# Keys and values in pieces within the attention of the first pair of head groups, the second pair's queries in DRAM

## The chip, the cores and the metric

The kernel runs on one core of one Trainium2 chip. A core has a matrix engine (TensorE, PE in the profile, with its weight loads as PEld), three other engines (VectorE: DVE, ScalarE: ACT, GpSimd: POOL), a queue engine that only issues transfers here (SyncE: SP), an on-chip memory (SBUF), and eight banks of accumulators (PSUM) that PE writes and that DVE and ACT read. Each engine runs its instructions in the order of its own list and waits at semaphores for the others. The metric is the device time of one launch in microseconds; lower is better.

## The reference, cut to what matters

One inference step of a trunk of two layers over T = 1056 tokens (1024 of a prompt, 32 of a sample), D = 1024. Layer 0 is an mLSTM with an MLP. Layer 1 is an attention over chunks of 64 tokens with an MLP. The change lies in that attention: 16 query heads in 4 groups, each group with one head of keys and values of 64 numbers. A chunk sees itself and the 8 chunks before it; the sample sees 512 cached keys and its own 32.

```python
kv = (x * (1 + kv_scale) + kv_shift) @ p['w_kv']          # 1024 -> 512
k_sh = kv[..., :KV_W].reshape(Bsz, S, NKV_B, HD_B)        # KV_W = 4 groups * 64
v_sh = kv[..., KV_W:].reshape(Bsz, S, NKV_B, HD_B)
q = (u @ p['w_q_b'][lb]).reshape(Bsz, S, NH_B, HD_B)      # 16 heads * 64
def one_chunk(args):                                       # prompt, per chunk ci
    s = jnp.einsum('bqkgd,bskd->bkgqs', qb, kb) * (HD_B ** -0.5) + bias
    s = jnp.where(valid, s, -jnp.inf)
    p = jax.nn.softmax(s, axis=-1)
    return jnp.einsum('bkgqs,bskd->bqkgd', p, vb)
...
y = o @ p['w_out_b'][lb]
```

The newest 512 keys and values of the prompt and the 32 of the sample are outputs as well (`k_p`, `v_p`, `k_s`, `v_s`).

## The kernel before, in words

Everything is float32. A product of two float32 matrices is made of three matmuls in a faster format: each operand is split into a high part (a cast by ACT, L89) and the rest (a subtraction by DVE, L90), and high·high, high·low and low·high are added up in PSUM (`proj`, L118 to L120).

**Queries (L1414 to L1440).** The tokens come in three blocks `TBS` of 384, 384 and 288. In two passes (column blocks `pr` 0, 1, 2, then 3) each block runs 24 matmuls for each of the `fc` of the pass (8 in all: two heads each) and splits the result by ACT (L1439) and DVE (L1440) into `QO`, one SBUF tile for each block. A block's inputs come out of a layer norm whose steps (`norms[ti]`, ACT L889 to L891 and L326 among them) run during the block ahead of it. `QO` later takes the attention's output in the queries' place.

**Keys and values (L1443 to L1527).** A phase of its own: 9 tiles of 128 tokens (`NT`; the last has 32). For a tile a transfer brings x (L1482), POOL multiplies (L1487), DVE adds (L1488), ACT and DVE split (L89, L90) into `uk`, and PE runs 24 matmuls for the keys and 24 for the values, in two PSUM banks (L1509 to L1511). Values are copied out by ACT (L1515). Keys go through `put_keys` (L1456 to L1467): a split (ACT L1456, DVE L1457), four transposes on PE into a bank `kt` (L1462), and eight casts out of that bank into the key tiles `k`, four by ACT for the high part and then four by DVE for the low part (L1467). Four tiles of cached keys go the same way (`kt_c`). In this phase the PSUM banks are in rotation for all of it.

**Attention (L1530 to L1660).** Head groups go in two pairs, `gp` 0 and 1. For a pair, 17 chunks (chunk 16 is the sample) come in an order that alternates wide and slim ones, and each chunk has two groups `e`. A softmax unit (`softmax_unit`) is the scores `s` on PE (L1558; 8 matmuls of 288 columns for a full chunk and group, in two units), bias and minimum by DVE (L1569), the exponential by ACT (L1572), a reciprocal by DVE (L1573) and the scaling by POOL (L1574). `transposed` turns the rows on PE into up to three banks `pt` (L1588), copied out to `pT` by DVE for e = 0 (L1598) and by ACT for e = 1 (L1596). `weighted_values` makes 20 matmuls `pv` (L1608) and writes the split result to `QO` (ACT L1613, DVE L1614). PSUM here: `s` 2 buffers of 2 banks, `pt` 3 buffers, `pv` 1. The position bias comes by transfers at the start of the attention (L1541, L1545).

**Order.** `Flow.tick` interleaves generators: a group's scores come three steps ahead of its transposes, and these one ahead of `pv`. On PE this order is taken as written (`manual_schedule`); on the other engines a scheduler sets a fixed order when the program is built.

Of the kernel before, what the change touches and what calls it, by code (L numbers as in the profile page):

```python
# [15 lines left out]
P = 128  # L16
# [59 lines left out]
def trunk_kernel(ctx: ExitStack, tc: tile.TileContext, a, o):  # L76
# [1332 lines left out]

    qo_cm, QOT = [], []  # L1410

    def qo(c):
        return QOT[c // 6][:, :, :, c % 6, :]
    wq = a["w_q_b"][0]  # L1414
    for gi, grp in enumerate(((0, 1, 2), (3,))):
        ws = {pr: [wblock(f"q{pr}_{half}", wq, 512 * half, 256 * pr) for half in range(2)] for pr in grp}
        for ti, (t0, n) in enumerate(TBS):
            if gi == 0:
                flow.finish(norms[ti])
                acc_cm[ti].__exit__(None, None, None)  # L1420
                qo_cm.append(tc.tile_pool(name=f"qo{ti}", bufs=1, reuse_waits="tile"))
                QOT.append(qo_cm[ti].__enter__().tile([P, 2, 2, 6 if ti < 2 else 5, 256], F32R, name=f"QO{ti}"))
                if ti == 2:
                    nc.vector.memset(qo(16)[:, :, :, 128:256].bitcast(F32), 0.0)
            for fc in [f for pr in grp for f in (2 * pr, 2 * pr + 1)]:
                g, r = fc // 2, 2 * (fc % 2)
                gp, e = g // 2, g % 2
                ps = mm(f"q_{fc}_{t0}")
                proj(ps[:, :n], n, ws[fc // 2], fc % 2, lambda hl, k: uap(hl, k, t0, n))
                for hd in range(2):  # L1430
                    for off, m, cnd in segs(t0, n):
                        if cnd == 0:
                            dst = QOT[ti][:, e, gp, 0:m // 64, (r + hd) * 64:(r + hd + 1) * 64]
                            src = ps[64 * hd:64 * hd + 64, off:off + m].rearrange("p (c i) -> p c i", i=64)
                        else:
                            dst = qo(16)[:, e, gp, (r + hd) * 32:(r + hd + 1) * 32]
# [5 lines left out]
    up_cm.__exit__(None, None, None)  # L1442

# [5 lines left out]
    wkv = [[wblock(f"kv{pr}_{half}", a["w_kv"], 512 * half, 256 * pr) for half in range(2)] for pr in range(2)]  # L1449
# [3 lines left out]
    def put_keys(src, m, pos, nm):  # L1453

        kd = [tmp_t([P, 256], f"kd{i}_{nm}", F32R) for i in range(2)]
        nc.scalar.copy(kd[0][:m], src)  # L1456
        nc.vector.tensor_sub(kd[1][:m], src, kd[0][:m].bitcast(F32))  # L1457
        yield
        ps = bank(f"kt_{nm}").rearrange("p (i b t) -> p i b t", i=2, b=2)
        for i in range(2):  # L1460
            for b in range(2):
                nc.tensor.transpose(ps[:, i, b, :m], kd[i][:m, b * P:(b + 1) * P].bitcast(F32), ident[:m, :m])  # L1462
        for i in range(2):
            for g0 in range(2):
                for half in range(2):
                    dst = kk[i][64 * half:64 * half + 64, g0::2, pos:pos + m]
                    KCOPY[i][half != g0](dst, ps[64 * g0:64 * g0 + 64, i, :, :m])  # L1467

# [23 lines left out]
    uks = [kv_input(0), kv_input(1)]  # L1492

    def cached_keys(t):
        cr = tmp_t([P, 256], f"ck_{t}")
        nc.sync.dma_start(cr, ck[t * P:(t + 1) * P])
        nc.sync.dma_start(V[:, 8 + t], cv[t * P:(t + 1) * P])
        yield 3.0
        yield from put_keys(cr, P, TP + t * P, f"c{t}")
    for t in range(NT):  # L1500
        if t % 2 == 0 and t < 8:
            flow.add(cached_keys(t // 2))
        m = P if t < NT - 1 else TS
        uk = uks[t]
        pk = [bank(f"kv{i}_{t}")[:, :256] for i in range(2)]
        for i in range(2):
            for k in range(KC):
                w = wkv[i][k // 4]
                nc.tensor.matmul(pk[i], uk[:, 0, k], w[:, 0, k % 4], start=(k == 0), stop=False)  # L1509
                nc.tensor.matmul(pk[i], uk[:, 0, k], w[:, 1, k % 4], start=False, stop=False)  # L1510
                nc.tensor.matmul(pk[i], uk[:, 1, k], w[:, 0, k % 4], start=False, stop=(k == KC - 1))  # L1511
            if i == 0:
                flow.tick()
        vi = t if t < NT - 1 else 12
        nc.scalar.copy(V[:m, vi], pk[1][:m])  # L1515
        flow.add(put_keys(pk[0][:m], m, t * P if t < NT - 1 else TP + 512, f"n{t}"))
        flow.tick()
        if t >= 4:
            ks = tmp_t([P, 256], f"ks_{t}")
            nc.scalar.copy(ks[:m], pk[0][:m])  # L1520
            dk, dv = (o["k_p"], o["v_p"]) if t < NT - 1 else (o["k_s"], o["v_s"])
            r0 = (t - 4) * P if t < NT - 1 else 0
            nc.sync.dma_start(dk[0, r0:r0 + m].rearrange("s g d -> s (g d)"), ks[:m])
            nc.sync.dma_start(dv[0, r0:r0 + m].rearrange("s g d -> s (g d)"), V[:m, vi])
        if t + 2 < NT:
            uks.append(kv_input(t + 2))
    flow.finish()  # L1527
    ps0.__exit__(None, None, None)


    at_cm = tc.tile_pool(name="attn", bufs=1, reuse_waits="tile")
    at = at_cm.__enter__()
    psT_cm = tc.tile_pool(name="psT", bufs=1, space=PSUM, reuse_waits="tile")
    psT = psT_cm.__enter__()
    bias, sbias = [], []
    for i, (nb, ns) in enumerate(((3, 0), (3, 0), (2, 1), (0, 3))):
        bt = ring.tile([P, 2112], F32, tag="wc", name=f"bias{i}", bufs=6)
        b3 = bt[:, :nb * 576].rearrange("p (b j) -> p b j", j=576) if nb else None
        for hd in range(2 if nb else 0):
# [7 lines left out]
        bias += [b3[:, j] for j in range(nb)]  # L1547
        sbias += [s3[:, j] for j in range(ns)]

    nun = [0]  # L1550

    def softmax_unit(qst, g, k0, nk, bt, off, nm):
# [3 lines left out]
        for b, j0, w in parts:  # L1556
# [3 lines left out]
        i = nun[0] % 12  # L1560
        p = tmp_t([P, 640], f"p_{nm}") if i < 5 else raw_tile([P, 640], f"p_{nm}") if i < 8 else \
            at.tile([P, 640], F32, tag="p", name=f"p_{nm}", bufs=4)
# [14 lines left out]
    def transposed(ps_, wid, e, nm):  # L1577
# [4 lines left out]
        for j0 in range(0, nt, 2):  # L1582
            pt = psT.tile([P, 2, 256], F32, tag="pt", name=f"pt_{nm}_{e}_{j0}", bufs=3)
            js = range(j0, min(nt, j0 + 2))
            for j in js:
# [7 lines left out]
            for j, m, kp in jss:  # L1593
                dst, src = pt_sb[:kp, j:j + m, :nq], pt[:kp, j - j0:j - j0 + m, :nq]
                if e:
                    nc.scalar.copy(dst, src)  # L1596
                else:
                    nc.vector.tensor_copy(dst, src)  # L1598
        return pt_sb
# [16 lines left out]
    def att_group(gp, c, e):  # L1616
# [3 lines left out]
        if c < 16:  # L1620
# [4 lines left out]
            pr_ = [softmax_unit(qo(c)[:, e, gp, pr * P:(pr + 1) * P], g, k0, nk, bias[2 * g + pr][:, 576 - nk:], off,  # L1625
                                f"{nm}_{e}{pr}") for pr in range(2)]
        else:
            wid, vt0 = 544, 8
            pr_ = [softmax_unit(qo(16)[:, e, gp, 0:P], g, TP, 544, sbias[g], 0, f"{nm}_{e}")]
        yield  # L1630
        yield
        yield
        pts[gp, c, e] = transposed(pr_, wid, e, nm)
        yield
        if e:
            if c < 16:
                dst = lambda hl: qo(c)[:, hl, gp, :]
            else:
                dst = lambda hl: qo(16)[:, hl, gp, :].rearrange("p (r i) -> p r i", i=64)[:, :, :TS]
            weighted_values(gp, [pts[gp, c, i] for i in range(2)], len(pr_) * P, wid, vt0, dst, nm)  # L1640
    pts = {}
# [8 lines left out]

    wide, slim = (8, 12, 13, 14, 15, 9, 10, 11), ((7, 6, 5, 4, 16, 3, 2, 1, 0), (16, 7, 6, 5, 4, 3, 2, 1, 0))
    with tc.manual_schedule(engines={mybir.EngineType.PE}):
        for gp in range(2):
            for i in range(17):
                c = slim[gp][i // 2] if i % 2 else wide[i // 2] if i < 16 else slim[gp][8]
                for e in range(2):
                    flow.add(att_group(gp, c, e))
                    flow.tick()  # L1660
                if gp and i in (8, 11):
                    wo_pre[0, len(wo_pre)] = wo_block(0, len(wo_pre))
        flow.finish()
    psT_cm.__exit__(None, None, None)
# [36 lines left out]
    def o_mov(hl, k, ti):  # L1701
        return QOT[ti][:, hl, k // 4, :, (k % 4) * 64:(k % 4 + 1) * 64]
# [96 lines left out]
```

## Time and profile before

| | |
|---|---|
| time, median of 3 runs | 2478.24 us (2475.82 to 2480.36) |
| the profiled execution's own time | 2479.81 us |
| its span in the trace | 2478.0 us |
| mean granted clock of PE | 0.992 |
| busy share of the span | PE 97%, PEld 93%, DVE 71%, ACT 41%, POOL 7% |
| queries, 1264 to 1359.2 us | 95.2 us, PE busy 94.5 |
| keys and values, 1359.2 to 1421.8 us | 62.6 us, PE busy 58.5 |
| attention, 1421.8 to 1632 us | 210.2 us |
| first scores of the second pair | at 1529.7 us |

The stages follow each other in time, so a window of the trace is a stage. "Busy" of PE counts a pipelined matmul from its start to its modelled end, so that a busy PE isn't yet a PE at its best pace. The idle time of an engine that isn't the one that sets the end costs nothing. A releaser is the instruction of another engine for which a wait ended.

### The profile page before, as it was taken

Reading aid. Unit: us, or ns where it says so; the run is one execution under the profiler, and the core shown is the slowest. Engines: PE = TensorE matmul, PEld = TensorE weight load, DVE = VectorE, ACT = ScalarE, POOL = GpSimd, SP = SyncE. Lnnn points to the kernel's source line nnn. Section 1 sums busy time; section 2 is a strip of 40 time slices with the busy share of each in tenths; the row PEclk is TensorE's granted clock in tenths of the full one; section 3 lists DMA queues with packets and bytes.
Section 4 is the critical chain, followed back from the end, with each engine's and each line's share of the span. In section 5 each row is a group of like instructions: output and inputs, shape, how many; then the busy total and the mean of one; then the engine's idle time right before and its main releaser. Section 6 shows DMA issues by size and latency. Waiting matters only on the chain.

```text
span 2478.0 us, 42688 instructions
## 1 busy us (share of the span) xinstructions
PE 2413.7 (97%) x16844; PEld 2315.4 (93%) x16844; DVE 1759.7 (71%) x4038; ACT 1016.9 (41%) x2118; POOL 168.6 (7%) x315
## 2 busy tenths in 40 slices
PE   7999999999999999999999999999999999999997
PEld 4999999999999999999999867789999999899997
DVE  4899999788679679677597667746853442776758
ACT  4644456382211212212266556654754443221212
POOL 0211100000000000000001134410000000000003
PEclk9999999999999999999999989999999999999999
DMA  8433224313224224234122310050375646767632
GB/s 297 122 110 101 84 88 129 107 35 119 77 87 137 84 86 135 80 92 142 43 98 82 91 40 1 18 147 27 134 251 212 215 179 254 262 239 273 255 130 72
DMA packets 236220, 318.10 MB, mean 128 GB/s; under 512 B 11624, under 2 KB 185084, under 8 KB 234996
## 3 DMA queue, kind: packets, MB, share of 16 engines
q1 hardware_dynamic: 236020, 315.38, 38.8%
q8 instruction: 132, 2.16, 0.4%
q14 instruction: 68, 0.56, 0.1%
HBM read 242.79 MB, written 74.91 MB: 128 GB/s over the span
## 4 chain that ended last, share of the span: by engine, by line
PE 78%; DVE 8%; DMA 6%; ACT 2%; issue 1%; POOL 0%; SPq 0%; DVEq 0%; POOLq 0%; ACTq 0%
PE up L118 10%; PE up L120 10%; PE up L119 9%; PE dn L1283 9%; PE dn L119 5%; PE dn L118 5%; PE dn L120 5%; DMA fx<-hd 3%; PE pv L1608 2%; PE pt L1588 2%; PE s L1558 2%; PE o L118 1%; PE o L119 1%; PE o L120 1%; PE op_b L118 1%
## 5 line engine op out<-in xcount | busy, mean ns | idle before, releaser
L120 PE MATMUL up<-u,w_up 128*128 128x264 f32 x1024 | 292.9, 286 | 0.0
L118 PE MATMUL up<-u,w_up 128*128 128x264 f32 x1024 | 292.4, 286 | 0.0
L119 PE MATMUL up<-u,w_up 128*128 128x264 f32 x1024 | 291.1, 284 | 0.0
L1283 PE MATMUL dn<-fx,wf 128*128 128x264 f32 x2208 | 275.3, 286 | 7.9 <-DMA fx<-hd 7.4
L1283 PEld LDWEIGHTS dn<-fx,wf 128*128 128x128 f32 x2208 | 272.2, 189 | 9.7 <-issue 4.6
L119 PE MATMUL dn<-h,w_dn 128*128 128x384 f32 (+1 forms) x768 | 249.5, 325 | 0.0
L118 PE MATMUL up<-U,w_up 128*128 128x384 f32 (+1 forms) x768 | 249.2, 324 | 0.0
L119 PE MATMUL up<-U,w_up 128*128 128x384 f32 (+1 forms) x768 | 247.9, 323 | 0.0
L118 PE MATMUL dn<-h,w_dn 128*128 128x384 f32 (+1 forms) x768 | 247.8, 323 | 0.0
L120 PE MATMUL up<-U,w_up 128*128 128x384 f32 (+1 forms) x768 | 247.6, 322 | 0.0
L120 PE MATMUL dn<-h,w_dn 128*128 128x384 f32 (+1 forms) x768 | 247.3, 322 | 0.0
L119 PEld LDWEIGHTS up<-u,w_up 128*128 128x128 f32 x1024 | 193.9, 189 | 0.0
L118 PEld LDWEIGHTS up<-u,w_up 128*128 128x128 f32 x1024 | 193.8, 189 | 0.0
L120 PEld LDWEIGHTS up<-u,w_up 128*128 128x128 f32 x1024 | 193.3, 189 | 0.0
L986 DVE SCALAR_TENSOR_TENSOR ACC<-dn,ada,ACC 128x264 f32<-128x264 f32 (+4 forms) x328 | 131.7, 426 | 86.4 <-PE dn L1283 74.6
L238 DVE SCALAR_TENSOR_TENSOR aacc<-rada,cs,aacc 128x256 f32<-128x256 f32 x448 | 190.3, 477 | 0.0
L986 DVE SCALAR_TENSOR_TENSOR acc<-dn,ada,acc 128x384 f32<-128x384 f32 (+2 forms) x256 | 119.4, 486 | 47.4 <-PE dn L120 46.3
L1025 ACT ACTIVATE r<-up 128x384 f32<-128x384 f32 (+1 forms) x96 | 44.3, 463 | 246.9 <-PE up L120 238.4
L119 PEld LDWEIGHTS dn<-h,w_dn 128*128 128x128 f32 x768 | 144.4, 188 | 0.2 <-DVE h L1028 0.2
L120 PEld LDWEIGHTS dn<-h,w_dn 128*128 128x128 f32 x768 | 144.5, 188 | 0.0
L120 PEld LDWEIGHTS up<-U,w_up 128*128 128x128 f32 x768 | 144.3, 188 | 0.0
L118 PEld LDWEIGHTS up<-U,w_up 128*128 128x128 f32 x768 | 144.2, 188 | 0.1
(354 smaller groups left out, 5957.4 us busy)
## 6 DMA issues: line engine op xcount, KB each, us to landing
hd<-HL SPq DMA_DIRECT2D x28, 1848.0 KB
raw_up<-in_w_up_dram SPq DMA_DIRECT2D x68, 512.0 KB
rada<-in_w_ada_dram SPq DMA_DIRECT2D x64, 512.0 KB
fx<-hd SPq DMA_DIRECT2D x37, 528.0 KB
raw_dn<-in_w_down_dram SPq DMA_DIRECT2D x36, 512.0 KB
ada_room<-in_w_ada_dram SPq DMA_DIRECT2D x32, 512.0 KB
fx<-hd SPq DMA_DIRECT2D x50, 264.0 KB
fx<-hd SPq DMA_DIRECT2D x16, 792.0 KB
```

What stands on the lines that cost most here:

```text
L118: nc.tensor.matmul(ps, wh, mov(0, k), start=(k == 0), stop=False)
L119: nc.tensor.matmul(ps, wh, mov(1, k), start=False, stop=False)
L120: nc.tensor.matmul(ps, wl, mov(0, k), start=False, stop=(k == nk - 1))
L238: nc.vector.scalar_tensor_tensor(acc[:, cnd], raw[:, k], sc, acc[:, cnd], op0=ALU.mult, op1=ALU.add)
L986: nc.vector.scalar_tensor_tensor(xs, ps[:, off + o:off + o + mm_], gate[:, fc, cnd:cnd + 1], xs, op0=ALU.mult, op1=ALU.add)
L1025: nc.scalar.activation(r, ps[:, :n], AF.Relu)
L1283: nc.tensor.matmul(p, ws[w][:, wl, k], t[:, s0, xl], start=first and k + n_ == 0, stop=k == kg - 1 and n_ == 2, skip_group_check=not first)
L1558: nc.tensor.matmul(s[:, b, :w], qst, kk[i][:, g, k0 + j0:k0 + j0 + w], start=(i == 0), stop=(i == 1))
L1588: nc.tensor.transpose(pt[:kp, j - j0, pr * P:(pr + 1) * P], ps_[pr][:, j * P:j * P + kp], ident)
L1608: nc.tensor.matmul(pv[64 * e:64 * e + 64, :nq], V[:kp, vt0 + j, g * 64:(g + 1) * 64], pts[e][:kp, j, :nq], start=(j == 0), stop=(j == nt - 1))
```

## The change

The two passes of the queries take the column blocks 2, 3, 0 and then 1, so that the second pair's queries (`fc` 4 to 7) are ready first in each block. `QO`'s layout puts the pair first. After `fc` 7 of each block the second pair's half of `QO` is written to DRAM (`qd`, 1.57 MB, 1.57 MB and 1.31 MB), and that half's room then holds the split weights of the keys and values. The phase of keys and values is gone: its matmuls come from a generator in pieces of 6, and each `put_keys` is a piece as well. 18 pieces (tiles 0 and 1) are placed ahead of the attention; the rest is handed out at three places per group in the first pair, 0.75 of a piece each, and ahead of a chunk whose keys are still missing. Both halves of a tile's result, keys and values, lie in one bank `KVB`. The transposes of keys share the buffers `pt` with the attention's, two while there are pieces left, three after. The first pair goes through its chunks from 0 up; the second pair keeps its order. When the pieces are at an end, `second_pair` loads the queries back and brings two further bias tiles; at the start only two are loaded.

```diff
     def qo(c, gp):
+        return QOT[c // 6][:, gp, :, c % 6, :]
-    for gi, grp in enumerate(((0, 1, 2), (3,))):
+    for gi, grp in enumerate(((2, 3, 0), (1,))):
...
+                if fc == 7:
+                    nc.sync.dma_start(qd[ti], QOT[ti][:, 1].bitcast(F32))
                 flow.tick(n / 96)
+            if gi:
+                if ti == 0:
+                    r0 = rooms(0, 3)
+                    kv_block(0, 0, r0[0:2])
+                elif ti == 1:
+                    r1 = rooms(1, 3)
+                    kv_block(0, 1, r1[0:2])
+                    kv_block(1, 0, (r0[2], r1[2]))
+                else:
+                    kv_block(1, 1, rooms(2, 2))
...
+    KVB = psX_cm.__enter__().tile([P, 2, 256], F32, name="KVB")
...
     def put_keys(kd, m, pos, nm):
-        ps = bank(f"kt_{nm}").rearrange("p (i b t) -> p i b t", i=2, b=2)
+        ps = psT.tile([P, 2, 256], F32, tag="pt", name=f"kt_{nm}", bufs=2).rearrange("p i (b t) -> p i b t", b=2)
...
+    def kv_tile(t):
...
+        for i in range(2):
+            pk = KVB[:, i]
+            for k in range(KC):
+                w = wkv[i, k // 4]
+                nc.tensor.matmul(pk, uk[:, 0, k], w[0][:, k % 4], start=(k == 0), stop=False)
+                nc.tensor.matmul(pk, uk[:, 0, k], w[1][:, k % 4], start=False, stop=False)
+                nc.tensor.matmul(pk, uk[:, 1, k], w[0][:, k % 4], start=False, stop=(k == KC - 1))
+                if k % 2 == 0:
+                    continue
+                if k == KC - 1 and i == 0:
+                    work = raw_tile([P, 4, 256], f"kd_{t}")
+                    kd = kd_of(work)
+                    split_keys(kd, pk[:m], m)
...
+                elif k == KC - 1:
+                    nc.scalar.copy(V[:m, vi], pk[:m])
...
+                    if t + 2 < NT:
+                        uks[t + 2] = kv_input(t + 2)
+                yield
+                if k == 3 and i == 1:
+                    put_keys(kd, m, pos, f"n{t}")
+                    yield
...
+    fills = [0, 18.0]
+    def fill(share):
...
+        fills[1] += share
+        while fills[0] < fills[1]:
+            if next(pieces, fill) is fill:
+                fills[0] = None
+                return
+            fills[0] += 1
...
+            if psY and nun[1] % 3 == 0:
+                pt = psY[0].tile([P, 2, 256], F32, tag="pt3", name=f"pt_{nm}_{e}_{j0}", bufs=1)
+            else:
+                pt = psT.tile([P, 2, 256], F32, tag="pt", name=f"pt_{nm}_{e}_{j0}", bufs=2)
             js = range(j0, min(nt, j0 + 2))
+            if j0 == 4:
+                fill(0.75)
...
+    def second_pair():
+        psX_cm.__exit__(None, None, None)
...
+        for ti in range(3):
+            nc.sync.dma_start(QOT[ti][:, 1].bitcast(F32), qd[ti])
+        bias_tile(2)
+        bias_tile(3)
...
-    wide, slim = (8, 12, 13, 14, 15, 9, 10, 11), ((7, 6, 5, 4, 16, 3, 2, 1, 0), (16, 7, 6, 5, 4, 3, 2, 1, 0))
+    order = tuple(range(17)), (8, 16, 12, 7, 13, 6, 14, 5, 15, 4, 9, 3, 10, 2, 11, 1, 0)
```

Three places in the engines' lists show what moved. A row has the line, the operation, what it writes and what it reads; a number behind a name tells buffers of one name apart.

The first place is PE in the first pair, where the keys of tile 6 (`kt_n_15372`) are put. Of the changed kernel:

```order
L1550 MATMUL KVB<-QO_13199,uk_14907 128x256
L1501 MATMUL kt_n_15372<-ident,kd_15303 128x128 x4
L1671 MATMUL pt_9_1_0_15386<-ident,p_9_10_15227 128x128
L1671 MATMUL pt_9_1_0_15386<-ident,p_9_11_15239 128x128
...
L1671 MATMUL pt_9_1_2_15392<-ident,p_9_10_15227 128x128
L1671 MATMUL pt_9_1_2_15392<-ident,p_9_11_15239 128x128
...
L1548 MATMUL KVB<-QO_13709,uk_14907 128x256
```

`kt`, `pt_9_1_0` and `pt_9_1_2` follow each other and share two buffers, so the third needs the buffer of the first; before, the key transposes stood among the matmuls of the key and value phase and had banks of that phase.

The second place is ACT at the same point, in the changed kernel: the exponentials of chunk 10, the four casts of the high part of tile 6's keys, then chunk 9's copies.

```order
L1649 ACTIVATE p_10_10_15349,mx_10_10_15350<-p_10_10_15349,mx_10_10_15350 128x576
L1649 ACTIVATE p_10_11_15360,mx_10_11_15361<-p_10_11_15360,mx_10_11_15361 128x576
L1506 CAST k_14124<-kt_n_15372 64x2x128 x4
L1679 COPY pT_9_1_15385<-pt_9_1_0_15386 128x512
L1493 CAST ck_15515<-ck_15515 128x256
L1679 COPY pT_9_1_15385<-pt_9_1_2_15392 128x512
```

Before, ACT had in the middle of the first pair only exponentials, `pT` copies and the writes to `QO`; now the casts of keys stand between two exponentials and the copies out of `pt`.

The third place is ACT in the queries, at the end of the layer norm of the third block. Before:

```order
L889 ACTIVATE w_n_2_13415<-var_n_2_13412,eps_ln 128x288
L1439 CAST QO_13196<-q_0_13440 64x6x64
L890 ACTIVATE w_n_2_13415<-w_n_2_13415 128x288
L891 ACTIVATE w_n_2_13415<-w_n_2_13415 128x288
```

and now:

```order
L889 ACTIVATE w_n_2_13419<-var_n_2_13416,eps_ln 128x288
L1458 CAST QO_13199<-q_0_13444 64x6x64
L890 ACTIVATE w_n_2_13419<-w_n_2_13419 128x288
L89 CAST QO_13199<-raw_kv_0_13979 128x1024
L891 ACTIVATE w_n_2_13419<-w_n_2_13419 128x288
```

The cast of a weight block into the room of the queries that go to DRAM now stands ahead of the norm's last step; it writes where the transfer to `qd` still reads.

More of the change, by code (lines that the diff above doesn't have):

```diff
@@ L1494, in cached_keys @@
     def cached_keys(t):
-        cr = tmp_t([P, 256], f"ck_{t}")
-        nc.sync.dma_start(cr, ck[t * P:(t + 1) * P])
+        work = raw_tile([P, 4, 256], f"ck_{t}")
+        nc.sync.dma_start(work[:, 2], ck[t * P:(t + 1) * P])
         nc.sync.dma_start(V[:, 8 + t], cv[t * P:(t + 1) * P])
[L1498 to L1526, printed above, removed]
@@ L1660, in trunk_kernel @@
                     flow.tick()
+                    if fills[0] is None and not psY:
+                        second_pair()
                 if gp and i in (8, 11):
```

125 lines of the change are left out of this document (92 added, 33 removed).

## The prediction

> **What bounds the kernel now.** I read first the stretches of the stages around the change (a row is a stretch, its length, and each engine's busy time with its instructions in brackets, then the granted clock of PE and the load on the transfers).
>
> ```profile
> core 0: us, PE busy (x) PEld busy (x) DVE busy (x) ACT busy (x) POOL busy (x), PEclk, DMA share, GB/s
> 1264.00:1359.20 95.20, 94.47 (x580) 93.01 (x580) 77.50 (x142) 62.32 (x134) 7.24 (x3) 1.00 0.30 94
> 1359.20:1421.80 62.60, 58.50 (x486) 57.55 (x485) 42.86 (x79) 34.31 (x88) 12.09 (x6) 1.00 0.35 91
> 1421.80:1440.00 18.20, 11.71 (x52) 8.88 (x51) 10.41 (x35) 8.87 (x25) 5.71 (x8) 0.70 0.65 149
> 1440.00:1480.00 40.00, 39.67 (x283) 29.29 (x282) 28.04 (x92) 24.51 (x67) 15.79 (x30) 0.96 0.00 1
> 1480.00:1520.00 40.00, 38.87 (x303) 29.06 (x302) 28.30 (x99) 26.18 (x75) 17.30 (x34) 1.00 0.01 1
> ```
>
> PE sets the end in all five, and only the attention's first 18.2 us stand out: 52 matmuls, at a clock of 0.70, where the next 40 us hold 283. The chain of work that ended last says why, and finer stretches show the clock behind it.
>
> ```profile
> 1423.54 6.78 DMA bias<-bias_d
> ```
>
> ```profile
> 1425.00:1430.00 5.00, 2.93 (x10) 2.04 (x10) 1.93 (x9) 2.50 (x6) 2.20 (x3) 0.58 1.02 223
> 1430.00:1435.00 5.00, 3.70 (x14) 3.23 (x15) 2.21 (x8) 2.39 (x6) 1.42 (x2) 0.50 1.02 228
> 1435.00:1440.00 5.00, 3.27 (x18) 2.37 (x17) 3.22 (x10) 2.90 (x7) 2.09 (x3) 0.84 0.07 18
> ```
>
> The transfer of the bias holds the first softmax up, and the clock then stays low for ten microseconds. The third view is the waits: in the key and value phase, and then from 1440 to 1530 us, the rest of the first pair.
>
> ```profile
> PE kv L1511 <- DVE uk L90: 4.1, 4, 2.1
> ```
>
> ```profile
> PEld s L1558 <- DVE mx L1569: 5.3, 15, 0.6
> PEld pt L1588 <- POOL p L1574: 3.5, 9, 0.4
> PEld pt L1588 <- DVE pT L1598: 2.0, 6, 0.4
> PE s L1558 <- DVE mx L1569: 1.2, 5, 0.3
> ```
>
> PE's own work, which the change leaves as it is, by the chain's steps of undisturbed matmuls and two rows of the timeline:
>
> ```profile
> 1375.20 0.12 PE kv L1509
> 1375.92 0.44 PE kt_c L1462 x4
> 1376.36 0.44 PE kt_n L1462 x4
> ...
> 1445.57 1.07 PE s L1558 x8
> 1446.64 0.87 PE pt L1588 x8
> ```
>
> ```profile
> 1504.24 2.38 PE L1608 MATMUL pv<-pT,V 128*64 128x256 f32 x20
> 1529.74 1.33 PE L1558 MATMUL s<-k,QO 128*128 128x288 f32 x8 [0.34 <-DVE mx L1569]
> ```
>
> Keys and values: 432 x 0.12 + 52 x 0.11 = 57.5 us. A pair, half of the 400 s, 500 pt and 520 pv of the attention: 200 x 0.134 + 250 x 0.109 + 260 x 0.119 = 85 us. The second row is the second pair's first scores: up to there, keys, values and the first pair took 1359.2 to 1529.7, 170.5 us, beside 143 of work. So 27 us are the most that this part can give.
>
> **What the change can give.** *The attention's start.* At the pace of the next row (283 matmuls in 40 us, 7.1 in a microsecond) 52 matmuls would take 7.3 us and not 18.2: 10.9 us. The two bias tiles are now issued in the queries, and key and value matmuls stand ahead of the first softmax. I count 11 (from 7, if the first softmax is late in its turn, to 12). *The waits of the key and value phase*: 4, PE's wait above. *The first pair's small waits*: the windows show 1.5 us of PE not busy in 80; the four rows of waits add up to 12.0, part of it under a matmul that still runs. Between 1.5 and 12 I take 8, near the upper end, since a late weight load also spreads the matmuls that count as busy. Gain: 11 + 4 + 8 = 23 us, if the pieces of keys and values fill these places and bring no waits with them.
>
> **What the change costs.** *The queries.* ACT's cast into the room of the written-out queries stands ahead of the last step of the third block's norm, and has to wait until the 1.57 MB to DRAM have been read. At the 228 GB/s of the row above that is 7 us from its issue. Before, the step came here:
>
> ```profile
> 1301.83 0.45 ACT L891 ACTIVATE w_n<-w_n 128x288 f32<-128x288 f32 x1
> ```
>
> ```profile
> PE q L118 <- ACT U L326: 0.2, 1, 0.2
> ```
>
> Queued behind the cast are that step and then all of the third block's inputs, which PE already waits for by 0.2 us, so that no slack covers it. Nought, if the transfer is issued by 1295, to 6; I take 2. The other transfers added to the queries run under PE's matmuls.
>
> *The start of keys and values.* Both halves of a tile now share a bank, so PE has to wait for the copies out of it, where it had another bank before. The groups of instructions of the phase (mean ns behind the comma):
>
> ```profile
> L1457 DVE TENSOR_TENSOR kd_n<-kv,kd_n 128x256 fp32r<-128x256 f32 (+1 forms) x9 | 3.8, 424 | 3.2 <-ACT kd_n L1456 3.0
> L1456 ACT CAST kd_n<-kv 128x256 fp32r<-128x256 f32 (+1 forms) x9 | 3.4, 373 | 20.1 <-DVE kd_c L1457 8.8 <-PE kv L1511 4.5 <-PE kt_c L1462 4.5
> L1515 ACT COPY V<-kv 128x256 f32<-128x256 f32 (+1 forms) x9 | 3.4, 373 | 3.2 <-PE kv L1511 3.2
> ```
>
> Between keys and values of a tile stand 0.37 + 0.42 us and two hand-overs, about 1.0; between values and the next keys 0.37 and its hand-overs, about 0.6. Up front nothing lies between: two of the first and one of the second, 2.6 us. The first softmax stands on DVE behind four key casts and a split (1.7 and 1.2 us by the rows below), of which I count 2.4. Together 5 (2 to 8). For the seven later tiles attention lies between most pieces: 7 x 1.6 = 11 us at most, of which I count 3 (0 to 7).
>
> *The keys among the transposes.* This is the largest term. The timeline of ACT and DVE (casts in a row are one row, with their time together), and one group:
>
> ```profile
> 1376.45 1.50 ACT L1467 CAST k<-kt_c 64x256 fp32r<-64x256 f32 x4
> 1377.97 1.51 ACT L1467 CAST k<-kt_n 64x256 fp32r<-64x256 f32 x4
> 1380.71 1.22 DVE L90 TENSOR_TENSOR uk<-x,uk 128x1024 fp32r<-128x1024 f32 x1
> 1382.30 1.72 DVE L1467 CAST k<-kt_c 64x256 fp32r<-64x256 f32 x4
> ```
>
> ```profile
> L1467 DVE CAST k<-kt_n 64x256 fp32r<-64x256 f32 x29 | 12.2, 421 | 2.1 <-ACT k L1467 1.8
> ```
>
> A bank of key transposes is read by ACT for 1.50 us, and then by DVE for 1.72: DVE's idle time ahead of its casts ends on ACT's. With a hand-over the bank is held 3.4 us from the end of the transposes; here kt_c was held from the end of its transposes at 1376.36 (the chain's row above) to 1384.02, over 7 us, because DVE was late, and it hurt nobody, since the phase had its other banks. Now two buffers serve keys and attention alike: the second bank behind the keys' is the keys' own again. PE has four transposes to do in between (0.44) and at some places six key and value matmuls (0.72), 0.4 to 1.2 us in all, and so waits 2.2 to 3.0 us if ACT begins at once. Where the exponentials of the next chunk stand ahead on ACT, they come on top, with their read-out:
>
> ```profile
> 1504.72 0.78 ACT L1572 ACTIVATE p<-p,mx 128x576 f32<-128x576 f32 x1
> 1505.40 0.19 ACT L1572 ACTIVATION_READ_ACCUMULATOR p<-p,mx 128x1 f32 x1
> ```
>
> Against it, in the early chunks the pieces and groups are small, and where the keys take the third bank of a group its scores and pv lie behind. Eleven such places are in the first pair (tiles 2 to 8 and four cached ones; the last tile has 32 tokens). Ten times 2.0 is 20 us; 6, if PE finds half a microsecond of wait at each, and 40, if two exponentials stand ahead at every one, are the ends.
>
> [...]
>
> *Two buffers for transposes, not three.* A copy out takes 0.55 us on DVE (mean) against 0.44 of transposes:
>
> ```profile
> L1598 DVE COPY pT<-pt 128x512 f32<-128x512 f32 (+3 forms) x82 | 42.9, 554 | 8.9 <-PE pt L1588 8.8
> ```
>
> The third bank of a group comes 0.3 us early unless a piece lies ahead, as it does at most groups; and DVE's casts make some copies late. 3 (1 to 8). *The hand-over.* 4.45 MB and two bias tiles (2.1 MB, worked out from their shapes as floats) come once the last piece is done. At 223 GB/s the first queries that are needed take 7 us and all of it 29; the second pair's first scores stand a chunk and a half of the first pair (8 to 10 us) and its bias later. I take 2 (0 to 10). Reads and writes of the outputs are in both versions.
>
> Costs: 2 + 5 + 3 + 20 + 3 + 2 = 35. Less the 23 gained: **+12 us**. On the profiled execution's own 2479.8 that is 2491.8; this execution was 1.6 us above the median, so on the median's scale **2490 us**.
>
> **Rivals.** *The fill works (faster).* The pieces cover the key casts, because PE comes to the third bank late anyway: then the keys cost 6, the shared bank 1, buffers 2, the start 3, queries and hand-over 1: 13 - 23 = -10, 2468 us. For it speaks that the attention's waits in the table are single ones of at most 0.6 us, against it that PE works in order and that ACT's casts are sandwiched between exponentials. It decides from below 0.7 us of wait per key place. *It evens out.* Key places at 0.8 us, 8 in all: 35 - 12 - 23 = 0, 2478 us. *DVE becomes the bound (slower).* The groups of DVE in the whole attention:
>
> ```profile
> L1569 DVE CUSTOM_DVE_ANT_0 p<-s,bias 128x576 f32<-128x576 f32 (+9 forms) x132 | 77.2, 604 | 16.2 <-PE s L1558 13.0 <-DMA bias<-bias_d 2.4 <-issue 0.3
> L1573 DVE RECIPROCAL mx<-mx 128x1 f32<-128x1 f32 x132 | 20.7, 160 | 29.2 <-ACT p L1572 27.8
> ```
>
> With copies (42.9), the writes to QO and the read-outs (24.2) they make 165 us, half of it for a pair; 82 + 43 of keys and values is 125 us beside 143 of PE. Against the 170.5 us of before: at the 71% that DVE shows in the attention's stretches 125 us take 176, and with the start, queries and hand-over (9) that is 185, +14; but if DVE's casts wait for ACT as its rows show (2.1 us of idle time ahead of 29 casts, 3.2 ahead of 9 splits) while its reductions wait behind them, 68% is nearer: 184 + 9, +22, 2500 us. It decides where PE's waits end on DVE's reductions and not on casts. *The reload isn't hidden (slower).* The first scores of the second pair wait 8 us more for the queries or the bias, and as after the bias stall above the clock falls (10.9 us were lost there for a wait of 6.8): +12 + 8, 2498 us. [...]
>
> **How the numbers follow.** The forecast has 0.38, the fill that works 0.24, evened out 0.17, DVE 0.12, the reload 0.09. About 0.2%, 5 us, is what a measurement of this kernel can tell from no change. The forecast's own range, 2482 to 2505, is the key places at 1.2 to 3.3 us. Over all, 8 in 10 lie between 2464 and 2506: down to the fill that works with a small rest, up to forecast and reload together. Faster 0.24, the same 0.18, slower 0.58.
>
> **What would show it.** Right: from the end of the queries to the second pair's first scores it takes about 180 us (before 170.5; PE's work is 143); in it PE waits for the casts out of kt (L1506) or for the copies behind them (L1679), some ten times, 1 to 4 us each; the start shows no bias wait and a full clock; the second pair keeps its 102 us. Wrong: PE's waits of that kind add up to under 8 us (then it's faster), or most of them end on DVE's reductions, or PE stands still ahead of the second pair's first scores.

## The result and the profile after

The changed kernel takes 2521.0 us (median, 2519.3 to 2525.4), the kernel before beside it 2479.3: four runs each, a ratio of 1.0173, with a 95% interval of 1.0155 to 1.0190. The forecast was slower, 2490 us in a range of 2464 to 2506. The sign was right; the time lies 15 us above the range, and the loss is 42 us where 12 were worked out.

The span grew from 2478.0 to 2519.3 us, and the trace says in which stage. The table counts from the first matmul of one stage to the first of the next, in the profiled executions, and the out-projection from its first matmul to its last; the attention's second pair starts with its 201st scores matmul. The median of all runs of a kernel stands beside it. The experiments stand in it as well, since they are read from it.

| profiled execution | queries | keys, values, first pair | second pair | out-projection | median us |
|---|---|---|---|---|---|
| before | 95.7 | 170.4 | 102.3 | 95.6 | 2479 |
| changed | 96.0 | 198.3 | 113.7 | 97.1 | 2521.0 |
| e1 softmax buffers | 96.0 | 199.6 | 105.0 | 95.6 | 2510.7 |
| e2 all ahead | 95.9 | 183.8 | 113.8 | 95.6 | 2505.7 |
| e3 low key casts left out | 96.0 | 186.7 | 114.4 | 97.2 | 2510.5 |
| e4 phase, with rooms | 95.8 | 156.9 | 102.2 | 95.6 | 2468.3 |
| e5 high key casts left out | 96.0 | 180.6 | 116.1 | 95.6 | 2503.7 |
| e6 cover | 95.9 | 186.0 | 115.2 | 95.6 | 2504.5 |
| e7 later input | 96.0 | 197.6 | 113.5 | 97.1 | 2518.9 |
| e8 rooms, rising order | 95.9 | 153.2 | 104.6 | 95.6 | 2467.9 |
| e9 = e1 + e6 | 95.9 | 182.2 | 104.7 | 95.6 | 2497.4 |
| e10 one bank in the phase | 95.9 | 178.9 | 102.3 | 95.6 | 2488.1 |

So +27.9 lie in keys, values and first pair, +11.4 in the second pair, which was to keep its time, +1.5 in the out-projection and +0.3 in the queries. First the stretches of the changed kernel (columns as in the prediction; the last row lies in the second pair).

```profile
core 0: us, PE busy (x) PEld busy (x) DVE busy (x) ACT busy (x) POOL busy (x), PEclk, DMA share, GB/s
1360.00:1380.00 20.00, 14.69 (x106) 14.08 (x105) 8.27 (x13) 5.83 (x16) 3.81 (x2) 0.91 0.30 80
1380.00:1400.00 20.00, 16.20 (x111) 14.10 (x110) 13.22 (x53) 11.82 (x40) 6.29 (x13) 0.91 0.21 54
...
1420.00:1440.00 20.00, 15.49 (x92) 11.90 (x93) 11.70 (x31) 9.51 (x26) 6.76 (x9) 0.83 0.06 16
...
1480.00:1500.00 20.00, 15.26 (x108) 12.56 (x106) 12.62 (x33) 11.46 (x30) 3.96 (x7) 0.91 0.07 21
...
1600.00:1640.00 40.00, 36.26 (x246) 26.48 (x244) 27.15 (x91) 22.68 (x64) 14.19 (x29) 0.91 0.12 27
```

No single stretch stands out as the attention's start did before. PE is idle for a tenth to a quarter of the time in nearly every stretch of the first pair, no other engine is busier than PE, and the granted clock is under 1 again and again. The waits of PE from 1390 us to the second pair's first scores, the five largest rows (what waits, what ended the wait, then us in total, how many, the longest):

```profile
PE pt L1671 <- ACT pT L1679: 14.5, 7, 3.2
PE pt L1671 <- DVE pT L1681: 4.4, 6, 1.6
PE KVB L1548 <- ACT kd L1558: 3.8, 2, 2.3
PE KVB L1548 <- DVE kd L1494: 1.7, 2, 1.2
PE pt L1671 <- DVE k L1506: 1.4, 2, 0.9
```

The first row is the place that the prediction named: transposes that wait for a buffer whose copy on ACT stands behind the casts of keys. One such place in the timeline, at tile 4's keys, shows the chain whole:

```profile
1451.99 0.66 PE L1501 MATMUL kt_n<-ident,kd 128*128 128x128 f32 x4
...
1452.68 0.74 ACT L1506 CAST k<-kt_n 64x256 fp32r<-64x256 f32 x2 [3.21 <-PE kt_n L1501]
...
1453.20 0.60 PE L1671 MATMUL pt<-ident,p 128*128 128x128 f32 x4
1453.45 0.78 ACT L1649 ACTIVATE p<-p,mx 128x576 f32<-128x576 f32 x1
1454.23 0.76 ACT L1649 ACTIVATE p<-p,mx 128x576 f32<-128x576 f32 x1
...
1455.10 0.75 ACT L1506 CAST k<-kt_n 64x256 fp32r<-64x256 f32 x2
...
1455.88 0.59 ACT L1679 COPY pT<-pt 128x512 f32<-128x512 f32 x1
1455.88 1.73 DVE L1506 CAST k<-kt_n 64x256 fp32r<-64x256 f32 x4 [0.61 <-ACT k L1506]
...
1456.51 0.66 PE L1671 MATMUL pt<-ident,p 128*128 128x128 f32 x4 [2.71 <-ACT pT L1679]
```

Of the keys' four casts on ACT two come before the next chunk's exponentials and two after; only then the copy out of the first bank of the group, which frees the buffer. PE's transposes at 1453.20 are done by 1453.8, and the next start at 1456.51. What follows such a wait was not in the forecast (stretches of 2 us; the third number from the end is the clock):

```profile
1454.00:1456.00 2.00, 0.00 (x0) 0.00 (x0) 0.45 (x3) 1.94 (x7) 1.38 (x2) 1.00 0.13 46
1456.00:1458.00 2.00, 1.49 (x10) 1.49 (x11) 1.93 (x5) 1.35 (x3) 0.27 (x2) 0.81 0.00 0
1458.00:1460.00 2.00, 2.00 (x10) 1.87 (x8) 0.78 (x3) 1.32 (x2) 0.00 (x0) 0.50 0.19 65
1460.00:1462.00 2.00, 2.00 (x17) 1.16 (x16) 1.80 (x5) 1.74 (x4) 0.00 (x0) 0.84 0.00 1
```

The wait of 2.7 us is over at 1456.5, and from 1457.2 to 1460.7 PE works at half clock: 1.7 us more are lost. Of the eight waits of over 2.2 us in this part, seven are followed by such a fall.

### The profile page after: what moved, and what is told of

Read it like the earlier page. It is cut to its first block, busy times and chain, and to the rows that moved or that the text cites. A ratio compares the mean times of both kernels' runs of the same rounds, so it can differ in the third digit from the quotient of the medians.

```text
span 2519.3 us, 42704 instructions
## 1 busy us (share of the span) xinstructions
PE 2429.6 (96%) x16844; PEld 2328.0 (92%) x16844; DVE 1761.8 (70%) x4039; ACT 1019.5 (40%) x2118; POOL 165.5 (7%) x315
## 4 chain that ended last, share of the span: by engine, by line
PE 80%; DVE 6%; DMA 5%; ACT 3%; issue 1%; POOL 0%; SPq 0%; ACTq 0%; DVEq 0%; POOLq 0%
PE up L118 10%; PE up L120 10%; PE up L119 10%; PE dn L1283 8%; PE dn L119 5%; PE dn L118 5%; PE dn L120 5%; DMA fx<-hd 4%; PE pv L1693 2%; PE s L1635 2%; PE pt L1671 2%; PE op_a L118 1%; PE op_a L119 1%; PE op_a L120 1%; PE o L118 1%
```

## The experiments

The theory after this reading had three parts: the key casts between the attention's copies (the key places), the bank that keys and values share, and something of its own in the second pair. The rivals were that the rising order, DVE's load or the reload did it. The reload could be put aside from the trace: the second pair's first scores follow the work ahead of them without a wait, and no wait of PE in that pair ends on a transfer.

**e1: the second pair's softmax buffers.** The second pair's waits, changed kernel against before, had one new row:

```profile
PE pv L1693 <- ACT pT L1679: 6.1, 2, 3.1
```

and the timeline at the first of the two waits shows what ACT waits for:

```profile
1612.69 1.33 SPq L96 DMA_DIRECT2D raw_ob<-in_w_out_b_dram  x2
...
1617.84 1.04 ACT L89 CAST w_ob<-raw_ob 128x1024 fp32r<-128x1024 f32 x1 [0.66 <-DMA raw_ob<-in_w_out_b_dram]
1618.79 0.85 ACT L1679 COPY pT<-pt 128x512 f32<-128x512 f32 x2
...
1619.42 2.82 PE L1693 MATMUL pv<-pT,V 128*64 128x256 f32 x10 [3.13 <-ACT pT L1679]
```

The weights of the out-projection are asked for in the second pair, into one of three buffers which softmax rows use too. The change gave these rows another turn (units 9 to 11 of 12, before 5 to 7), so the buffer comes free one chunk later, and the cast stands on ACT ahead of the copies.

```diff
-        p = tmp_t(...) if i < 5 else at.tile(...) if i < 9 else raw_tile(...)
+        p = tmp_t(...) if i < 5 else raw_tile(...) if psY and i < 8 else at.tile(...)
```

> In the second pair the softmax rows take the buffers in the order of the kernel before (units 5 to 7 of 12 the three that they share with raw weights, 8 to 11 the pool's own); in the first pair nothing is changed. Theory: the changed kernel's second pair takes 113.7 us and not 102.3 because the out-projection's weights wait for one of those three buffers and their cast stands ahead of the copies that pv needs (PE waits of 3.4 and 3.2 us), and the clock falls behind them. Then the second pair comes back to 102 to 104 us and the time to 2508 to 2513 us. Rival: the second pair is slower because of its third transposes' buffer, which now takes turns in a fixed way, or because of the reload: then the two waits stay and so does 2521.

Measured: 2510.7 us (2508.3 to 2515.2), 10.4 under the changed kernel, as expected; the second pair took 105.0 us, one more than the 102 to 104 expected, and of the out-projection's 1.5 us all came back. The first request now goes out here (a row for seven of them):

```profile
1608.10 54.48 SPq L96 DMA_DIRECT2D raw_ob<-in_w_out_b_dram  x7
```

which is 48.0 us after the second pair's first scores; in the changed kernel it was 54.4. No wait of PE over 0.7 us is left in that pair. So a quarter of the loss has nothing to do with keys and values: it is a renumbering of buffers, one swapped line of the change.

**e2: all keys and values ahead.**

```diff
-    fills = [0, 18.0]
+    fills = [0, 99.0]
```

> All pieces of keys and values are placed ahead of the attention; the shared bank, the two buffers for key transposes, the rooms, the early bias and the first pair's rising order stay. Theory (the harm comes from mixing: casts of keys on ACT and DVE between the attention's copies, with PE's order fixed): ahead of the attention 57 us of matmuls, some 1.6 us of bank waits for each of 9 tiles, key transposes beside nothing else, about 75 us; then a first pair with three buffers of 90 to 95 us; with the second pair's 11 as it is, 2490 to 2498 us. Rival (the shared bank and the rising order alone cost it): 2515 or more.

Measured: 2505.7 us (2503.9 to 2510.6), between the two. From the first matmul of keys to the first scores it took 88.1 us where I had said about 75; the first pair after it 95.6, where before the attention's first pair alone took 107.6 with the bias stall. So the rising order isn't the harm, and mixing costs 14.5 us (198.3 against 183.8) although the pieces should have covered waits. But the part ahead is far too long, and its waits, in the stretch up to the first scores, are all at the one bank:

```profile
PE KVB L1548 <- ACT kd L1558: 9.2, 5, 3.7
PE KVB L1548 <- DVE kd L1494: 8.4, 4, 3.7
PE KVB L1548 <- ACT V L1561: 3.0, 5, 1.0
```

**e3 and e5: the key casts of one engine left out.** e3 leaves out DVE's four casts, e5 ACT's; each lacks that part of the keys.

```diff
+    nc.gpsimd.memset(kk[1].bitcast(F32), 0.0)      # e5: kk[0]
...
-        for i in range(2):
+        for i in range(1):                          # e5: range(1, 2)
```

> DVE's four casts of the keys' low part are left out for every tile (the low part of the keys is set to zero once), so that this part of the computation is missing; transposes, ACT's casts and all orders stay. Theory: a bank of key transposes is then held 1.7 us in place of 3.4, and the ten waits of PE behind it, with the falls of the clock that follow four of them, mostly go: 2495 to 2503 us. Rival (ACT's casts behind the exponentials hold the bank, DVE's don't matter): not under 2512. Rival (DVE's load sets the pace): the reductions' waits shrink too, and it falls under 2490.

> The mirror of e3: ACT's four casts of the keys' high part are left out for every tile (the high part is set to zero once, so that this part of the computation is missing), DVE's four stay. After e3, which took 0.6 us from each wait of PE at a key place and left about 2 us. Theory (it is ACT's queue that holds the transposes' buffers: key casts behind two exponentials and ahead of the copies out of pt): without them the waits at the key places fall under 1 us, first pair and keys from 198 us to 176 to 184, time 2500 to 2507 us. Rival (what holds them is the exponentials themselves, or DVE): the waits stay at 2 us, and it ends as e3 did, at 2510 or above.

Measured: e3 2510.5 us (2509.0 to 2515.6), e5 2503.7 (2499.4 to 2505.1); the first pair 186.7 and 180.6 us. e3 missed its theory's 2495 to 2503 and came out near the rival: the time from one transposes to the next fell by only 0.6 us at a key place, as PE now waits for ACT's casts themselves. The waits from 1390 us on, of e3 and then of e5 (an edit shifts the line numbers behind it; L1507 is the changed kernel's L1506):

```profile
PE pt L1672 <- ACT k L1507: 11.6, 6, 2.6
```

```profile
PE pt L1672 <- ACT pT L1680: 6.3, 6, 1.7
PE pt L1672 <- DVE pT L1682: 4.6, 5, 2.7
PE KVB L1549 <- ACT kd L1559: 3.8, 2, 2.2
```

e5 lies in its theory's ranges: without ACT's casts the waits on ACT's copies are 6.3 us in place of 14.5, and none is over 1.7, where under 1 was expected. It isn't DVE's load: taking its casts away leaves 11.6 us of waits on ACT. The longer hold is ACT's list, casts and exponentials together. Each run saves more than its waits: 11.6 and 17.7 us of keys, values and first pair, against 7.3 and 9.4 us less of PE's waits there (36.3 in the changed kernel, 29.0 and 26.9). Most of the rest is the clock: one minus the granted clock, summed over that part, is 13.6 us in the changed kernel, 9.2 in e3 and 6.2 in e5, so 4.4 and 7.4 less.

**e6 and e9: more of PE's work behind the key transposes.**

```diff
-                yield
+                if not (k == 5 and i == 1):
+                    yield
                 if k == 3 and i == 1:
                     put_keys(kd, m, pos, f"n{t}")
-                    yield
...
-    fills = [0, 18.0]
+    fills = [0, 14.0]
```

(`fill(0.75)` is `fill(0.55)` at its places; behind cached keys the next tile's piece follows at once. e9 has e1's edit as well.)

> After each group of key transposes 12 matmuls of keys and values follow at once on PE (one piece with them; before, none or 6), and the other places hand out 0.55 of a piece in place of 0.75; nothing else is changed. Theory: PE has 1.4 us more to do while casts hold the bank, so that each wait shrinks by 0.7 to 1.4 us and most of the clock's falls behind them go: first pair and keys 198 us to 184 to 190, time 2507 to 2513 us. Rival (the copies of the group itself wait behind the casts on ACT, whatever PE does in between): 2518 or more.

> e1 and e6 together: the second pair's softmax rows in the buffers of before, and 12 matmuls of keys and values after each group of key transposes. Theory (two terms apart from each other, 10.4 us in the second pair and the out-projection, 16.6 in the first): 2492 to 2497 us; the second pair back at 102 to 106 us. Rival (both recover one and the same loss, such as a clock that a later wait lowers again): 2500 to 2504.

Measured: e6 2504.5 us (2504.1 to 2508.4), 16.6 under the changed kernel and 2.5 below the expected range; first pair 186.0, as expected. With the copies covered (the transposes' waits on ACT's copies are 2.5 us), what PE waits for from 1390 us on is the hold of the key transposes' bank itself, to the last cast on DVE:

```profile
PE pt L1670 <- DVE k L1506: 10.5, 7, 2.5
```

e9 2497.4 (2491.5 to 2500.1), the second pair 104.7: 23.6 under, where the two edits alone add up to 26.9. The upper end of the expectation is just missed, and the runs spread over 9 us; the two terms are apart, as the stages in the table show (the first pair gains in e6, the second in e1, both in e9), but I can't tell whether the last 3 us are scatter. With both mended it is still 18.8 us slower than before.

**e7: the start.** At the start PE waited 3.8 us for the split of tile 1's keys, which on DVE stood behind tile 2's input.

```diff
+                    if t == 1:
+                        uks[2] = kv_input(2)
...
-                    if t + 2 < NT:
+                    if 0 < t and t + 2 < NT:
```

> The input of tile 2 is asked for after tile 1's keys are split and not after tile 0's values, so that on DVE tile 1's split stands ahead of tile 2's input. Theory: PE's wait of 3.9 us for that split at the start becomes about 1.1, and the clock's fall behind it (1.7 us) goes: 2515 to 2518 us. Rival (the start only hands the wait on: tile 2's input is late, or the first softmax): 2520 or more.

Measured: 2518.9 us (2512.8 to 2521.9), 2 us less and within the scatter. The time lies between the theory's and the rival's; the waits speak for the rival, the wait went on. PE's waits up to 1390 us, of the changed kernel and then of e7:

```profile
PE KVB L1548 <- DVE kd L1494: 4.8, 2, 3.8
PE s L1635 <- DVE mx L1646: 3.0, 1, 3.0
```

```profile
PE s L1637 <- DVE mx L1648: 5.3, 1, 5.3
PE KVB L1548 <- DVE kd L1494: 2.5, 3, 1.0
```

7.8 us in the changed kernel, 7.8 in e7: DVE has splits, inputs and key casts of two tiles and the first softmax to do there, and what isn't late for one is late for the next.

**e4, e8 and e10: what the room is worth, and what the bank costs.** (In e4's diff, against the changed kernel, the phase of before is put back in the place of the pieces, with its weights read from the rooms.) e4 takes from the change only the second pair's queries in DRAM, the weights in their room and the early bias. Keys and values are a phase as before, with banks in rotation, and the attention is as before; queries and two bias tiles come back at its start. e8 is e4 with the first pair's chunks in rising order, e10 is e4 with keys and values in the halves of one fixed bank (the key transposes then take the other banks in a set turn, which the lines below don't show):

```diff
+    uks = [kv_input(0), kv_input(1)]
     bias_tile(0)
     bias_tile(1)
+    for t in range(NT):
...
+                w = wkv[i, k // 4]
...
+    for ti in range(3):
+        nc.sync.dma_start(QOT[ti][:, 1].bitcast(F32), qd[ti])
+    bias_tile(2)
+    bias_tile(3)
```

```diff
-                c = slim[gp][i // 2] if i % 2 else wide[i // 2] if i < 16 else slim[gp][8]      # e8
+                c = i if not gp else slim[gp][i // 2] if i % 2 else wide[i // 2] if i < 16 else slim[gp][8]
```

```diff
-        pk = [bank(f"kv{i}_{t}")[:, :256] for i in range(2)]
+        pk = [KVB[:, 256 * i:256 * i + 256] for i in range(2)]      # e10; KVB is one tile
```

> Keys and values as a phase of their own with banks of their own, and the attention's order, buffers and banks, all as in the kernel before; of the change stay the second pair's queries in DRAM, the weights in their room, and the first two bias tiles early; queries and the other bias tiles come back at the attention's start. Theory: this alone keeps the gain at the attention's start (11 us by the forecast, less what the first softmax needs anyway) and has none of the costs: 2468 to 2473 us. Rival (the first softmax is late anyway, the bias was only the last of several): 2476 to 2480.

> e4 with the first pair's chunks in rising order, as the changed kernel has them. In e2 the first pair took 95.6 us in this order with three buffers for transposes, in e4 98.6 in the old order. Theory (the order itself does no harm, the narrow chunks first let the start fill quicker): 2463 to 2467 us. Rival (narrow chunks leave the softmax's latency open): 2470 or more, and the rising order is a part of what the change costs.

> e4 with one fixed bank for keys and values of all tiles (a half each), as in the changed kernel; key transposes keep banks in rotation, all else is e4. Theory (the shared bank costs by itself: 1.0 us between a tile's halves and 0.6 to the next tile, in e2 with DVE's order 30 us for nine tiles): the phase 58 us in e4 to 73 to 88, time 2483 to 2498 us. Rival (in e2 it was the key transposes in two buffers): not above 2475.

Measured: e4 2468.3 us (2467.1 to 2472.7), ratio to before 0.9958 (0.9946 to 0.9971): faster than both kernels by 10.9 and 52.7 us. e8 2467.9 (2465.3 to 2468.7), ratio 0.9952 (0.9939 to 0.9964): no difference to e4 that can be told, so the expected gain of the order didn't show, and it does no harm either. In the table, one profiled execution each, the order takes 3.7 us from the first pair and adds 2.4 to the second, about what e1, in the same order, has over before (105.0 against 102.3). e10 2488.1 (2486.2 to 2490.4): 19.8 us for the shared bank, in the theory's range. The stretches of e4:

```profile
1360.76:1419.04 58.28, 57.74 (x486) 57.26 (x484) 43.73 (x79) 33.84 (x87) 8.22 (x4) 1.00 0.38 99
1419.04:1440.00 20.96, 19.11 (x128) 14.13 (x129) 16.90 (x57) 14.22 (x39) 10.32 (x18) 1.00 0.49 203
```

The phase runs without PE's waits for the input, and the attention starts at full clock: 128 matmuls in 21 us where before there were 52 in 18. And the waits of e10's phase up to 1438 us; in e4 the phase has one of 0.4 us:

```profile
PE KVB L1561 <- DVE kd_n L1488: 6.0, 2, 5.4
PE kt_n L1494 <- ACT kd_n L1487: 4.5, 8, 1.1
PE kt_n L1494 <- DVE kd_n L1488: 2.0, 1, 2.0
PE KVB L1561 <- ACT ks L1572: 1.0, 2, 0.5
```

13.5 us of waits, and 22.0 in the stage; 5.1 more went with the clock, which fell behind the waits of 5.4 and 2.0. The two rows on kt_n say where some of the waits come from: with one bank, the next tile's first half begins only when the copies are through, and the key transposes that stood among its matmuls come before their split is done.

## Why the prediction was wrong, by its own steps

Three steps failed: the shared bank was priced at about half of its waits, the second pair was put at no change, and the clock that falls behind PE's waits was in none of the costs.

**The key places, +20 from 6 to 40: right in place, and near in size by other numbers.** The mechanism is that of the timeline above: ACT's list of casts and exponentials, not DVE's casts alone. The prediction had the bank's hold as 1.50 + 1.72 us one after the other, with exponentials "on top"; e3 and e5 show that the exponentials and ACT's casts weigh more than DVE's. In the changed kernel the transposes' waits for ACT's copies and for DVE's casts are 14.5 + 1.4 = 15.9 us in the first pair. But they aren't ten waits of 2.0: five of the eleven places have one of 2.5 to 3.2 us, and all other waits of these rows make 2.4. That the sum is near is in part luck. The clock fell behind four of the five, 6.8 us more, which the sum didn't have.

**The shared bank, +5 at the start and +3 later: the step that was too small.** Of these 8, 2.4 were the first softmax and 5.6 the bank. In the changed kernel PE's waits at the bank are 4.8 + 0.6 before 1390 us and 5.5 after, 11 us, and the clock fell behind the two longest (3.8 and 2.3 us), 5.1 us more. e10 prices the bank at 22 us in a phase by itself, e2's waits at 20.6; no run gave the changed kernel a second bank. The forecast counted the copies alone, 0.37 + 0.42 and two hand-overs, as if ACT and DVE began at once. They have a list too, as the longest of the later waits shows:

```profile
1420.02 0.37 ACT L1493 CAST kd<-KVB 128x256 fp32r<-128x256 f32 x1
1420.28 0.68 ACT L1649 ACTIVATE p<-p,mx 128x448 f32<-128x448 f32 x1
...
1420.94 0.67 ACT L1649 ACTIVATE p<-p,mx 128x448 f32<-128x448 f32 x1
...
1421.59 0.36 ACT L1558 COPY kd<-KVB 128x256 f32<-128x256 f32 x1
...
1422.01 0.39 PE L1548 MATMUL KVB<-QO,uk 128*128 128x256 f32 x1 [2.28 <-ACT kd L1558]
```

It ended on a third copy on ACT, the one for the output, behind two exponentials; the forecast had left that copy out of the hold altogether. The prediction took the reads of one bank by ACT and by DVE one after the other, 1.50 and 1.72 us at the key casts; at the two halves of this bank PE and the copies came one after the other too: the first matmul of the second half waited 2.28 us for the last copy out of the first.

**The first pair's small waits, -8: gone from their rows, but no gain can be shown.** The four rows that the prediction added up to 12.0 us are 4.2 in the changed kernel from 1390 us on:

```profile
PEld pt L1671 <- DVE pT L1681: 3.9, 5, 1.0
PEld s L1635 <- DVE mx L1646: 0.3, 1, 0.3
```

The waits for the softmax fell from 10.0 us to 0.3, and those for DVE's copies rose from 2.0 to 3.9. Most of the 10.0 were waits of weight loads, in part beside running matmuls; PE itself stood still for 1.2 of them. So what they were worth in time stays open, and so does what removed them: the pieces between, or the longer waits for copies ahead, behind which a softmax is ready. No run separates the two.

**The attention's start and the input waits, -15: right in size, but not for this kernel.** In e4 keys, values and first pair take 156.9 us where before they took 170.4, 13.5 less. The changed kernel spends it again at once: from the first key matmul to the first scores it takes 20.0 us for 12.4 us of work (96 x 0.12 + 8 x 0.11), then 3.0 us more for the first softmax, with two falls of the clock where a full clock was forecast. e7 shows that it isn't one late instruction.

**The second pair, "keeps its 102 us": wrong, 113.7.** This term wasn't in the sum. The swapped line of the softmax rows' buffers was put at nothing; e1 shows that it costs 10.4 us, 6.1 of them as waits at pv and the rest with the clock and the out-projection.

**Queries +2, reload +2, two buffers +3:** 0.3 was measured for the queries, and the reload left no wait at all. For the buffers, the waits on DVE's copies are 4.4 us at `pt` and 1.4 at `kt_c`.

In sum, by PE's waits and by one minus the granted clock in the two profiled executions: in keys, values and first pair PE waited 36.3 us where before it waited 12.2, and lost 13.6 to the clock where before it lost 6.8. That is 31 us more, for the 27.9 by which the part grew; the forecast had 8 for it. The bank is 16 of this with its clock falls, against 5.6 worked out. The second pair and the out-projection add 12.9 which the sum didn't have, and queries and reload take 3.7 off it. (A fall of the clock is put down here to the wait just ahead of it.) Of the rivals, DVE as the bound and the reload were both named as slower and neither happened; whether the fill works with banks of its own stays open, since no run gave it any.

## What to carry to other kernels

Ask of work that is to fill another stage's waits which buffers it brings of its own (that it then pays wasn't run): here two stages shared two PSUM buffers and two engines' lists, and each handed its latencies to the other, while the part of the change that only freed room (e4) was worth 10.9 us by itself. Price a shared buffer with the lists of the engines that empty it, not with the copies' durations. And when a diff gives a rotating buffer another turn, look for everybody else who takes from the same ring, also in a stage that the change doesn't mean.

## What the runs showed that was not expected

Waits of PE of about 2 to 4 us were followed by a clock of 0.50: in the changed kernel behind seven of eight waits of over 2.2 us in keys, values and first pair, for 3.4 us at six of them and for 6.8 us at one, in e3 behind waits of 1.9 and 2.1 us. The length of a wait alone doesn't tell. A wait of 2.5 us that ended at 1434.2 wasn't followed by a fall, nor one of 2.9 us that ended at 1642.9 in the second pair, nor in the kernel before the 2.1 us of its key and value phase, behind which the clock stayed at 1.00.

The traces of the kernel before and of the changed one show more. Every change of the granted clock in them lies on a grid of 3.41 us (in the changed kernel it falls at 1375.32, 1385.56, 1423.10 and 1457.24 us, whole multiples apart), and each of the ten falls from the first key matmul to the out-projection, two before and eight in the changed kernel, follows an interval of the grid in which PE was busy for 0.22 to 1.92 us. The wait that ended at 1434.2 and the one that ended at 1456.5, each with the interval behind it (columns as before; after the length comes PE's busy time):

```profile
1429.93:1433.34 3.41, 1.75 (x15) 1.51 (x13) 1.07 (x6) 2.70 (x8) 0.87 (x2) 1.00 0.02 5
1433.34:1436.75 3.41, 2.57 (x18) 1.98 (x20) 2.60 (x7) 2.51 (x6) 0.41 (x1) 1.00 0.03 10
...
1453.82:1457.24 3.42, 0.73 (x6) 0.73 (x7) 1.71 (x8) 2.92 (x9) 1.55 (x3) 1.00 0.11 37
1457.24:1460.65 3.41, 3.41 (x18) 2.94 (x18) 1.96 (x5) 2.37 (x4) 0.10 (x1) 0.50 0.12 38
```

The first wait lies across a step of the grid and leaves both intervals more than half busy, the second lies in one interval. In these two traces, over the same stretch, five intervals at full clock have PE busy for under 1.55 us, and each is followed by one at 0.50; of 11 with 1.55 to 1.9 us, four are; of 139 with more, one. So the waits of over 2.2 us in keys, values and first pair cost 1.7 us of clock (half of 3.41) on top of themselves at six places and 3.4 at one, where the clock stayed low for two intervals, and none at the eighth. That it depends on where a wait falls on the grid is read from the traces; no run moved a wait alone.
